# Accumulated low parts, 128-column causal matmuls and GpSimd-issued moves in a two-layer attention and recurrence trunk

## Chip, cores and metric

The kernel runs on one core of a Trainium2 chip. The metric is the device time of one execution in microseconds (us). The engines are TensorE (PE, with its weight loads listed as PEld), VectorE (DVE), ScalarE (ACT), GpSimd (POOL) and SyncE (SP).

## What is computed

Two layers over 256 tokens of width 1024, in float32. Cut to what matters:

```python
h = rmsnorm(x, norm_g[l])
q, k, v, ga, iq, ik, iw, xr, gr, ma, mb = jnp.split(h @ w_in[l], offsets, axis=-1)
q, k, iq, ik = rotary position encoding of each
# indexer: 16 heads of 64, one shared key
dots = jnp.einsum('bqhd,bsd->bqhs', iqb, ik)
idx_score = jnp.einsum('bqh,bqhs->bqs', iwb, jax.nn.relu(dots))
idx_score = jnp.where(causal, idx_score, -inf); _, sel = lax.top_k(idx_score, 64)
# attention over the selected causal keys, 8 heads of 128
p = softmax(where(selected, q @ k.T * scale, -inf));  attn = p @ v
y_a = (attn * jax.nn.silu(ga)) @ w_out_attn[l]
xr = causal_depthwise_conv(xr, conv_w[l], conv_b[l])          # width 4
r, i = sigmoid(blockdiag(xr, w_rg) + b_rg), sigmoid(blockdiag(xr, w_ig) + b_ig)   # 16 blocks of 88
hr = associative scan of (exp(-8 r softplus(-lam)), sqrt(1 - a^2) * i * xr)
y_b = (hr * jax.nn.silu(gr)) @ w_out_rnn[l]
x = x + (sigmoid(ma) * y_a + sigmoid(mb) * y_b) @ w_o[l]      # after two layers: a last rmsnorm
```

## The kernel before

**Products.** Every float32 matrix product is made of three matmuls in the fp32r type: with w = wh + wl and x = xh + xl (a rounded high part and the rest), PE computes xh·wh, xl·wh and xh·wl. So each 128x128 block of weights is loaded and streamed against 256 token columns (or the other way about, with 512 weight columns) three times. The weights come in chunks of 8 blocks (512 KB). SP loads a chunk from DRAM into `raw` (`Stream.load`, line 519, 4 buffers); ACT, or now and then DVE, rounds it into `wh` (`copy`, lines 480 and 482); DVE subtracts, wl = raw − wh (`sub`, line 486). `wh` and `wl` are rings of 6 chunks each. `Stream.chunk` is the place.

**Order.** `Program` (from line 232) is a scheduler that runs when the kernel is built: each operation has a cost and a latency, and it writes out one fixed order for each engine. PE's order follows the units of `plan` (line 65), with parts shifted later by the LATE constants; the other engines go by deadlines that follow from PE's positions. Once built, an instruction waits for its data and for the instructions ahead of it on its own engine.

**A layer.** `plan` sets: the head unit (indexer key `ik`, head weights `iw`, three indexer query groups), the other indexer queries `iq`, then for each of 11 groups of recurrence channels the units xr, gr and gate, mixed with the gates ga, ma, mb; then four pairs of q, k (and twice v) with attention, then yb, ya and the output projection wo.

**The indexer.** `rotate` (line 773) makes the rotary encoding of the projection in PSUM: it first copies the 32-partition halves crosswise into `sw` (four ACT copies of 32x512 for `iq`, line 473), then two products and a sum on DVE. `queries` (line 853) splits the result `iqr` of two groups (four heads) into two stacks `iqs` of 128 partitions, one head's high part over its low part: two 64-row copies and two 64-row subtractions. `head` makes `kh` and `kl` of the key on rows 0 to 63 and again on 64 to 127. `dots` (line 871) multiplies a stack with kh and with kl, always over all 256 keys, for both halves t of the queries; ACT's relu into `rl` and DVE's weighted sum into `wk` follow, and POOL masks what is not causal. `select` finds the top 64.

**The gates.** The recurrence blocks are 88 wide and the tiles 128, so `gather` (line 975) collects the foreign rows of neighbouring tiles into `xf` and `xk` by SBUF-to-SBUF transfers that SP issues (line 991), between its weight loads; `gate` multiplies them.

**Attention.** `logits` (line 1082) multiplies q and k for both query halves over all 256 keys. `attend` (line 1108) transposes the three causal blocks of probabilities into `ptp`, splits them into `pth` and `ptl` of 512 columns whose first 128 are a zero block, and multiplies `v` with 256 columns for both key halves st, the zero block included. `v` (line 1067) is made in eight units before the first and third pair.

Of the kernel before, what the change touches and what calls it, by code (L numbers as in the profile page):

```python
# [64 lines left out]
def plan(l):  # L65
# [21 lines left out]
    for pr in range(4):  # L87
        u += [("q", 2 * pr), ("q", 2 * pr + 1), ("k", 2 * pr), ("k", 2 * pr + 1)]
        if pr % 2 == 0:
            u += [("v", pr // 2, c) for c in range(4)]  # L90
        u.append(("attn", pr))
# [56 lines left out]
NCH = -(-NBLK // 8)  # L148

# [76 lines left out]
ENGINES = ("pe", "act", "dve", "pool", "dma")  # L226
LATENCY = {"pe": 190.0, "act": 140.0, "dve": 130.0, "pool": 200.0, "dma": 2000.0}
# [4 lines left out]
class Program:  # L232
# [52 lines left out]
    def issue(self):  # L285
# [27 lines left out]
        table = None  # L313
        order = []
# [3 lines left out]
        while n < total:  # L318
# [19 lines left out]
            for h in o.new:  # L338
                k = (h.pool, h.tag)
                slots[k].pop(0)  # L340
                given[k][h.index] = True
                while nalloc[k] < len(given[k]) and given[k][nalloc[k]]:
                    nalloc[k] += 1
            o.start, o.end = s, s + cost
# [49 lines left out]
    def choose(self, e, cand, free, slots, nalloc, given, table, pepos):  # L394
# [3 lines left out]
        for o in cand:  # L398
# [15 lines left out]
            if e == "act" and o.tabs is not ANY and table not in o.tabs:  # L414
                pr += TABLE_LAG
                if o.prio[0] > pepos + URGENT:
                    s = max(s, o.ready + HOLD)
            key = (s if s > now else now, pr, o.no)
# [7 lines left out]
TABLE_LAG = 10000.0  # L426
URGENT = 8000.0
# [5 lines left out]
def trunk(ctx, tc, xT, pos, pre, par, fgb, wst, out):  # L433
# [34 lines left out]
    def act(o, i, func, **kw):  # L468
        c = (50 if i.psum() else 94) + 0.833 * o.size() + (200 if "accum_out" in kw else 0)
        aps = [kw[k] for k in ("scale", "bias") if isinstance(kw.get(k), V)]  # L470
        outs = [o] + ([kw["accum_out"]] if "accum_out" in kw else [])
        pg.op("act", c + 93 * len(aps), outs, [i] + aps,
              lambda: nc.scalar.activation(real(o), real(i), func, **{k: real(v) for k, v in kw.items()}),
              TABS.get(func))
# [39 lines left out]
    def trans(o, i):  # L514
        pg.op("pe", 70, [o], [i, ident], lambda: nc.tensor.transpose(real(o), real(i), real(ident)))
# [12 lines left out]
    class Stream:  # L528
# [23 lines left out]
        def chunk(self, c):  # L552
            if c not in self.parts:
# [14 lines left out]
                copy(wh, raw)  # L568
                sub(wl, raw, wh.bitcast(F32))
# [63 lines left out]
    for i in range(2):  # L633
        ph = const(f"pth{i}", [512], F32R)
        pl = const(f"ptl{i}", [512], F32R)
        pset(ph.bitcast(F32)[:, 0:128], 0.0)
        pset(pl.bitcast(F32)[:, 0:128], 0.0)
        pts.append((ph, pl))
# [133 lines left out]

    def rotate(o, ps, sw, tabs, step):
# [11 lines left out]
    class Layer:  # L785
        def __init__(self, l, xg, norm):
# [6 lines left out]
            self.rope = {}  # L793
            self.aT = []
# [14 lines left out]
        def head(self):  # L809
# [12 lines left out]
            rotate(ikr[:64], ps[:64], f1("sw")[:64], [t[:64] for t in self.ti], 32)  # L822
            mul(iwt, ps, R)
            kh, kl = self.kh, self.kl
            for b in (0, 64):
                copy(kh[b:b + 64], ikr[:64])
            for b in (0, 64):
                sub(kl[b:b + 64], ikr[:64], kh.bitcast(F32)[:64])
# [24 lines left out]
        def queries(self, i):  # L853

            iqr = f2("iqr")
            rotate(iqr, self.banks["iq"], f2("sw"), [t.twice() for t in self.ti], 32)
            st = [r2("iqs") for _ in range(2)]
            for a in range(2):
                s = slice(64 * a, 64 * a + 64)
                copy(st[a][s], iqr[s])  # L860
            for a in range(2):
                s = slice(64 * a, 64 * a + 64)
                d = slice(64 - 64 * a, 128 - 64 * a)
                sub(st[a][d], iqr[s], st[a].bitcast(F32)[s])
# [6 lines left out]
        def dots(self, i, st, t):  # L871

            pg.late = LATE_DOTS
            ps = bank("pq", "dots")
            for a in range(2):
                w = st[a][:, t * P:t * P + P]
                mm(ps[:, a, :], w, self.kh, True, False)
                mm(ps[:, a, :], w, self.kl, False, True)
            pg.late = 0.0
            n = P * (t + 1)  # L880
# [94 lines left out]
        def gather(self, kind, rows):  # L975
# [8 lines left out]
            else:  # L984
                dst = pg.tile(fp, "f1", [P, T], F32R, nm("xk"), F1)
                for h in range(2):
# [3 lines left out]
            pg.op("dma", 300 * len(moves), [dst], list(src.values()),  # L990
                  lambda: [nc.sync.dma_start(real(o.bitcast(F32)), real(i.bitcast(F32))) for o, i in moves][-1])
# [75 lines left out]
        def v(self, n, c):  # L1067
            ps = self.by_token("v", self.h[2 * c:2 * c + 2], c == 0, c == 3)
            if c == 3:
                self.vt = []  # L1070
                for t in range(2):
                    self.vt.append((r2("vh").join(), r2("vl").join()))
                    split(self.vt[t], ps[t])
# [8 lines left out]
        def logits(self, hd):  # L1082
# [3 lines left out]
            for t in range(2):  # L1086
                s = slice(t * P, t * P + P)
                mm(ps[:, t, :], qh[:, a, s], kh[:, a, :], True, False)
                mm(ps[:, t, :], qh[:, a, s], kl[:, a, :], False, False)
                mm(ps[:, t, :], ql[:, a, s], kh[:, a, :], False, True)  # L1090
# [17 lines left out]
        def attend(self, hd, lts):  # L1108
            pg.late = LATE_LOG + LATE_TURN
            ps = bank("pt", "ptp").join()  # L1110
            for dst, lt, s in ((384, 1, 0), (128, 1, P), (256, 0, 0)):
                trans(ps[:, dst:dst + P], lts[lt][:, s:s + P])
            ph, pl = pts[hd % 2]
            act(ph[:, P:], ps[:, P:], AF.Copy)
            sub(pl[:, P:], ps[:, P:], ph.bitcast(F32)[:, P:])
# [4 lines left out]
            for st in range(2):  # L1120
                vh, vl = self.vt[st]
                r = slice(256 - 256 * st, 512 - 256 * st)
                c = slice(a * P, a * P + P)
                for w, m in ((vh, ph), (vh, pl), (vl, ph)):
                    mm(ps, w[:, c], m[:, r], n == 0, n == 5)
# [194 lines left out]
```

## Time and profile before

| | |
|---|---|
| median of 3 runs | 706.12 us (705.9 to 706.37) |
| profiled execution | 705.1 us, of which the span in the profile is 703.3 us |
| PE busy | 686.1 us, 98% of the span, 4720 matmuls |
| DVE busy | 602.6 us, 86% |
| ACT busy | 482.8 us, 69% |
| POOL busy | 6.4 us, 1% |
| transfers | 125.24 MB, 178 GB/s mean |
| TensorE clock granted | 1.00 of 2.4 GHz throughout |

The profile is of one execution. "Busy" is time in which an instruction of that engine was running. A matmul's row has its start and a length; matmuls overlap, so the distance between two starts says how long one occupies PE. An arrow `<-` behind a wait names the engine and tile whose end released it.

### The profile page before, as it was taken

The numbers are of one execution on the slowest core, as the hardware profiler recorded it, in microseconds if no ns is written. First come the engines' busy times: TensorE is split into PE (matmuls) and PEld (weight loads), VectorE is DVE, ScalarE is ACT, GpSimd is POOL, SyncE is SP. The second block draws the span as 40 slices with busy tenths as digits, with TensorE's granted clock in tenths as the row PEclk, the third lists the DMA queues.
The fourth block names the chain that finished last, engine by engine and source line by source line (L and its number), as shares of the span: only waits on it lengthen the run. The fifth ranks groups of instructions, "written<-read, shape, count | busy, mean of one in ns | idle before, by whom it ended". The sixth has DMA issues, their size and how long they took to land.

```text
span 703.3 us, 12628 instructions
## 1 busy us (share of the span) xinstructions
PE 686.1 (98%) x4720; PEld 638.4 (91%) x4720; DVE 602.6 (86%) x1177; ACT 482.8 (69%) x775; POOL 6.4 (1%) x18
## 2 busy tenths in 40 slices
PE   7898999999999999999999999999999999999996
PEld 7898999999999998888999899999999898988885
DVE  7989999999897959857779997999989987796573
ACT  7996675799995748444558766588769765674433
POOL 0000000000000000000000000000000000000000
PEclk9999999999999999999999999999999999999999
DMA  8646566667756462655553655576666565535621
GB/s 292 195 157 211 159 197 201 203 189 220 223 177 189 149 192 75 205 180 179 173 173 111 213 178 163 177 220 207 210 205 185 182 190 163 180 101 171 195 73 60
DMA packets 38104, 125.24 MB, mean 178 GB/s; under 512 B 4892, under 2 KB 7260, under 8 KB 38044
## 3 DMA queue, kind: packets, MB, share of 16 engines
q1 hardware_dynamic: 38044, 124.44, 56.5%
q8 instruction: 37, 0.61, 0.3%
q14 instruction: 23, 0.19, 0.1%
HBM read 119.77 MB, written 1.05 MB: 172 GB/s over the span
## 4 chain that ended last, share of the span: by engine, by line
PE 82%; DVE 7%; ACT 6%; issue 2%; DMA 2%; SPq 0%; DVEq 0%; ACTq 0%
PE rps L512 14%; PE yb L512 9%; PE q L512 7%; PE k L512 7%; PE ops L512 6%; PE ma L512 6%; PE ya L512 6%; PE v L512 6%; PE gps L512 5%; PE ga L512 4%; PE mb L512 4%; DVE wl L486 2%; PE iq L512 2%; ACT wh L480 2%; PE lg L512 2%
## 5 line engine op out<-in xcount | busy, mean ns | idle before, releaser
L486 DVE TENSOR_TENSOR wl<-raw,wh 128x1024 fp32r<-128x1024 f32 x223 | 271.5, 1220 | 58.4 <-ACT wh L480 57.1
L480 ACT ACTIVATE wh<-raw 128x1024 fp32r<-128x1024 f32 x196 | 207.3, 1059 | 138.6 <-PE rps L512 21.4
L512 PE MATMUL rps<-hh,wh 128*128 128x256 f32 x352 | 99.5, 283 | 0.0
L512 PE MATMUL rps<-hl,wh 128*128 128x256 f32 x352 | 99.5, 283 | 0.0
L512 PE MATMUL rps<-hh,wl 128*128 128x256 f32 x352 | 99.5, 283 | 0.0
L512 PEld LDWEIGHTS rps<-hh,wl 128*128 128x128 f32 x352 | 67.4, 192 | 0.3
L512 PEld LDWEIGHTS rps<-hh,wh 128*128 128x128 f32 x352 | 67.3, 191 | 0.3
L512 PEld LDWEIGHTS rps<-hl,wh 128*128 128x128 f32 x352 | 67.4, 191 | 0.0
L512 PE MATMUL yb<-wh,g 128*128 128x512 f32 x176 | 59.0, 396 | 0.0
L512 PE MATMUL iq<-xg,wh 128*128 128x256 f32 x232 | 45.3, 285 | 0.0
L512 PE MATMUL ya<-wh,aT 128*128 128x512 f32 x128 | 40.8, 395 | 0.0
L512 PE MATMUL ga<-hh,wh 128*128 128x256 f32 x128 | 36.3, 283 | 2.0 <-DVE iwt L486 2.0
L512 PEld LDWEIGHTS iq<-xg,wh 128*128 128x128 f32 x232 | 37.4, 192 | 0.0
L512 PEld LDWEIGHTS yb<-wh,g 128*128 128x128 f32 x176 | 32.5, 188 | 5.3
L512 PE MATMUL q<-hh,wl 128*128 128x256 f32 x128 | 36.4, 284 | 0.0
L512 PE MATMUL q<-hh,wh 128*128 128x256 f32 x128 | 36.3, 284 | 0.0
L512 PE MATMUL ga<-hl,wh 128*128 128x256 f32 x128 | 36.3, 283 | 0.0
L512 PE MATMUL k<-hh,wl 128*128 128x256 f32 x128 | 36.3, 283 | 0.0
L512 PE MATMUL q<-hl,wh 128*128 128x256 f32 x128 | 36.2, 283 | 0.0
L512 PE MATMUL ga<-hh,wl 128*128 128x256 f32 x128 | 36.2, 283 | 0.0
L512 PE MATMUL k<-hh,wh 128*128 128x256 f32 x128 | 36.2, 283 | 0.0
L512 PE MATMUL k<-hl,wh 128*128 128x256 f32 x128 | 36.2, 283 | 0.0
(264 smaller groups left out, 1944.6 us busy)
## 6 DMA issues: line engine op xcount, KB each, us to landing
raw<-in_wst_dram SPq DMA_DIRECT2D x224, 512.0 KB, 4.0
xk<-xs SPq DMA_DIRECT2D x24, 48.0 KB, 3.5
out_dram<-z SPq DMA_DIRECT2D x4, 256.0 KB, 2.3
rah<-in_wst_dram SPq DMA_DIRECT2D x2, 256.0 KB
xr<-in_xT_dram SPq DMA_DIRECT2D x1, 512.0 KB
fg<-in_fgb_dram SPq DMA_DIRECT2D x2, 256.0 KB
xk<-xs SPq DMA_DIRECT2D x8, 40.0 KB
xf<-xs SPq DMA_DIRECT2D x2, 160.0 KB
```

Of the source, the lines that this page charges most:

```text
L480: lambda: nc.scalar.activation(real(o), real(i), AF.Copy),
L486: lambda: nc.vector.tensor_tensor(real(o), real(a), real(b), op=op))
L512: lambda: nc.tensor.matmul(real(o), real(w), real(m), start=start, stop=stop, skip_group_check=grp))
```

## The change

The line numbers of the rows below that are headed "now" are of the changed kernel.

- **Low parts.** For 38 of the weight chunks (every third one before the first q of each layer, 19 a layer; `SUMMED`) DVE no longer subtracts. ACT writes wl = −raw, rounded, and a transfer that GpSimd issues loads the same chunk from DRAM a second time and adds it to wl on arrival.
- **128 columns.** `dots` and `logits` of query half t = 0 multiply the first 128 keys only, and `attend` multiplies key half st = 1 with the second 128 queries only. The zero block of `pth` and `ptl`, and its four memsets, are gone.
- **Indexer.** `rotate32` copies the projection once (ACT, 128x512) and swaps the 32-row quarters by four transfers on GpSimd's queue. `queries` makes one copy and one subtraction of 128x512 and moves 64-row halves by three transfers; `kh` and `kl` are made once and moved to the other 64 rows by two.
- **Gathers.** The gates' transfers are issued by GpSimd instead of SP.
- **v.** The second four v units go between the units of pair 1 instead of behind those of pair 2.
- **Scheduler.** A kind of operation "sum" for the transfers on GpSimd, costs of 2000 and 700 a transfer and a latency of 3500; PE's matmuls are given at least 110 each less a reserve of up to 60, and short ones are pushed apart; a transpose counts 112 instead of 70.

```diff
         u += [("q", 2 * pr), ("q", 2 * pr + 1), ("k", 2 * pr), ("k", 2 * pr + 1)]
-        if pr % 2 == 0:
-            u += [("v", pr // 2, c) for c in range(4)]
+        if pr == 0:
+            u += [("v", 0, c) for c in range(4)]
+        if pr == 1:
+            u[-4:] = [w for c, w in enumerate(u[-4:]) for w in (("v", 1, c), w)]
...
+def summed_chunks():
+    out, n = set(), 0
+    for l in range(L):
+        early = sum(len(unit_blocks(u)) for u in plan(l)[:plan(l).index(("q", 0))])
+        out.update(range(n // 8 + 6, (n + early) // 8, 3))
+        n += sum(len(unit_blocks(u)) for u in plan(l))
+    return out
+SUMMED = summed_chunks()
...
 PSUM_TAGS = ("pp", "pq", "pt")
-ENGINES = ("pe", "act", "dve", "pool", "dma")
-LATENCY = {"pe": 190.0, "act": 140.0, "dve": 130.0, "pool": 200.0, "dma": 2000.0}
+ENGINES = ("pe", "act", "dve", "pool", "dma", "sum")
+LATENCY = {"pe": 190.0, "act": 140.0, "dve": 130.0, "pool": 200.0, "dma": 2000.0, "sum": 3500.0}
...
                     nalloc[k] += 1
+            if o.eng == "pe":
+                cost = max(cost, ISSUE - self.spare)
+                self.spare = min(max(self.spare + cost - ISSUE, 0.0), SPARE)
...
                     s = max(s, o.ready + HOLD)
+            if e == "pe" and o.cost < ISSUE:
+                pr += -SHORT if self.spare >= ISSUE - o.cost - 5.0 else SHORT
...
 TABLE_LAG = 10000.0
+ISSUE = 110.0
+SPARE = 60.0
+SHORT = 6000.0
...
     def trans(o, i):
-        pg.op("pe", 70, [o], [i, ident], lambda: nc.tensor.transpose(real(o), real(i), real(ident)))
+        pg.op("pe", 112, [o], [i, ident], lambda: nc.tensor.transpose(real(o), real(i), real(ident)))
...
                 wl = pg.tile(wp, "wl", [P, 1024], F32R, nm("wl"), WBUF)
-                copy(wh, raw)
-                sub(wl, raw, wh.bitcast(F32))
+                if c in SUMMED:
+                    pg.op("act", 94 + 0.833 * 1024, [wl], [raw],
+                          lambda: nc.scalar.activation(real(wl), real(raw), AF.Copy, scale=-1.0))
+                    copy(wh, raw)
+                    pg.op("sum", 2000, [wl], [wl],
+                          lambda: nc.gpsimd.dma_start(real(wl), wst[c], accum_op=OP.add))
+                else:
+                    copy(wh, raw)
+                    sub(wl, raw, wh.bitcast(F32))
...
+    def move(moves):
+        outs, ins = ({a.h: a for a in side}.values() for side in zip(*moves))
+        pg.op("sum", 700 * len(moves), list(outs), list(ins),
+              lambda: [nc.gpsimd.dma_start(real(o.bitcast(F32)), real(i.bitcast(F32))) for o, i in moves][-1])
+    def rotate32(o, ps, sw, tabs):
+        n = o.shape[0]
+        act(o, ps, AF.Copy, also=(sw,))
+        move([(sw[b:b + 32], o[b ^ 32:(b ^ 32) + 32]) for b in range(0, n, 32)])
+        mul(o, o, tabs[0])
+        mul(sw, sw, tabs[1])
+        add(o, o, sw)
...
             ikr, iwt = f1("ikr"), f1("iwt")
-            rotate(ikr[:64], ps[:64], f1("sw")[:64], [t[:64] for t in self.ti], 32)
+            rotate32(ikr[:64], ps[:64], f1("sw")[:64], [t[:64] for t in self.ti])
...
             kh, kl = self.kh, self.kl
-            for b in (0, 64):
-                copy(kh[b:b + 64], ikr[:64])
-            for b in (0, 64):
-                sub(kl[b:b + 64], ikr[:64], kh.bitcast(F32)[:64])
+            split((kh[:64], kl[:64]), ikr[:64])
+            move([(t[64:], t[:64]) for t in (kh, kl)])
...
             iqr = f2("iqr")
-            rotate(iqr, self.banks["iq"], f2("sw"), [t.twice() for t in self.ti], 32)
-            st = [r2("iqs") for _ in range(2)]
-            for a in range(2):
-                s = slice(64 * a, 64 * a + 64)
-                copy(st[a][s], iqr[s])
-            for a in range(2):
-                s = slice(64 * a, 64 * a + 64)
-                d = slice(64 - 64 * a, 128 - 64 * a)
-                sub(st[a][d], iqr[s], st[a].bitcast(F32)[s])
+            rotate32(iqr, self.banks["iq"], f2("sw"), [t.twice() for t in self.ti])
+            one, low, two = r2("iqs"), r2("iql"), r2("iqs")
+            split((one, low), iqr)
+            move([(two[:64], one[64:]), (two[64:], low[64:])])
+            move([(one[64:], low[:64])])
+            st = one, two
...
             ps = bank("pq", "dots")
+            n = P * (t + 1)
...
                 w = st[a][:, t * P:t * P + P]
-                mm(ps[:, a, :], w, self.kh, True, False)
-                mm(ps[:, a, :], w, self.kl, False, True)
+                mm(ps[:, a, :n], w, self.kh[:, :n], True, False)
+                mm(ps[:, a, :n], w, self.kl[:, :n], False, True)
             pg.late = 0.0
-            n = P * (t + 1)
...
                         moves.append((dst[d:d + z - a], src[i][a:z, h, :]))
-            pg.op("dma", 300 * len(moves), [dst], list(src.values()),
-                  lambda: [nc.sync.dma_start(real(o.bitcast(F32)), real(i.bitcast(F32))) for o, i in moves][-1])
+            move(moves)
...
             if c == 3:
-                self.vt = []
+                self.vt[n] = [(r2("vh").join(), r2("vl").join()) for _ in range(2)]
                 for t in range(2):
-                    self.vt.append((r2("vh").join(), r2("vl").join()))
-                    split(self.vt[t], ps[t])
+                    split(self.vt[n][t], ps[t])
...
             for t in range(2):
-                s = slice(t * P, t * P + P)
-                mm(ps[:, t, :], qh[:, a, s], kh[:, a, :], True, False)
-                mm(ps[:, t, :], qh[:, a, s], kl[:, a, :], False, False)
-                mm(ps[:, t, :], ql[:, a, s], kh[:, a, :], False, True)
+                s, n = slice(t * P, t * P + P), P * (t + 1)
+                mm(ps[:, t, :n], qh[:, a, s], kh[:, a, :n], True, False)
+                mm(ps[:, t, :n], qh[:, a, s], kl[:, a, :n], False, False)
+                mm(ps[:, t, :n], ql[:, a, s], kh[:, a, :n], False, True)
...
             ps = bank("pt", "ptp").join()
-            for dst, lt, s in ((384, 1, 0), (128, 1, P), (256, 0, 0)):
+            for dst, lt, s in ((2 * P, 1, 0), (0, 1, P), (P, 0, 0)):
                 trans(ps[:, dst:dst + P], lts[lt][:, s:s + P])
+            ps = ps[:, :3 * P]
             ph, pl = pts[hd % 2]
-            act(ph[:, P:], ps[:, P:], AF.Copy)
-            sub(pl[:, P:], ps[:, P:], ph.bitcast(F32)[:, P:])
+            act(ph, ps, AF.Copy)
+            sub(pl, ps, ph.bitcast(F32))
...
             n = 0
-            for st in range(2):
-                vh, vl = self.vt[st]
-                r = slice(256 - 256 * st, 512 - 256 * st)
+            for st, r in ((0, slice(P, 3 * P)), (1, slice(0, P))):
+                vh, vl = self.vt[hd // 4][st]
...
                 for w, m in ((vh, ph), (vh, pl), (vl, ph)):
-                    mm(ps, w[:, c], m[:, r], n == 0, n == 5)
+                    mm(ps[:, st * P:], w[:, c], m[:, r], n == 0, n == 5)
...
             mul(of, ps, self.sga[hd])
```

PE issues as many matmuls as before: 160 of them (32 of `dots`, 24 of `logits` and 24 of `attend` in each layer) go from 256 to 128 columns. POOL's list has 144 transfers in 163 rows where it had none in 22, SP's 239 rows instead of 307. DVE makes 185 subtractions into wl instead of 223 and rounds 49 chunks instead of 27, ACT 174 instead of 196.

On POOL, in layer 0, from the swap of the third pair of indexer query groups on, POOL's list is now as follows (sw: swapped quarters; iqs and iql: high and low parts; kh, kl: the key; wl: an accumulated low part). The memsets and masks of before had no transfer among them.

```order
L805 DMA sw_628<-iqr_614 32x512 x4
L805 DMA iqs_669<-iqs_623 64x512
L805 DMA iqs_669<-iql_657 64x512
L805 DMA sw_693<-iqr_680 32x512 x4
L805 DMA kh_710<-kh_710 64x256
L805 DMA kl_716<-kl_716 64x256
L805 DMA iqs_750<-iqs_673 64x512
L805 DMA iqs_750<-iql_707 64x512
L805 DMA iqs_623<-iql_657 64x512
L598 DMA wl_731<-in_wst_dram 128x1024
```

The first stack for `dots`, iqs_623, is complete only behind the two moves of the key and the two of the second pair's stack iqs_750.

On DVE, in the same stretch, the rows up to the key's low part kl were, before:

```order
L486 TENSOR_TENSOR iqr_629<-iqr_629,sw_531 128x512
L486 TENSOR_TENSOR wl_695<-raw_543,wh_603 128x1024
L486 TENSOR_TENSOR iqs_698<-iqr_629,iqs_698 64x512
L486 TENSOR_TENSOR iqs_704<-iqr_629,iqs_704 64x512
L486 TENSOR_TENSOR sw_311<-sw_311,si_518 64x256
L486 TENSOR_TENSOR iqr_726<-iq_505,ci_434 128x512
L486 TENSOR_TENSOR ikr_449<-ikr_449,sw_311 64x256
L486 TENSOR_TENSOR wl_733<-raw_566,wh_660 128x1024
L486 TENSOR_TENSOR kl_744<-ikr_449,kh_736 64x256
L486 TENSOR_TENSOR wl_751<-raw_607,wh_677 128x1024
```

and now:

```order
L511 TENSOR_TENSOR wl_636<-raw_468,wh_569 128x1024
L511 TENSOR_TENSOR iqr_474<-iqr_474,sw_509 128x512
L511 TENSOR_TENSOR iql_657<-iqr_326,iqs_623 128x512
L511 TENSOR_TENSOR ga_634<-ga_634,ga_461 128x512
L511 TENSOR_TENSOR sw_316<-sw_316,si_580 64x256
L511 TENSOR_TENSOR wl_683<-raw_548,wh_659 128x1024
L511 TENSOR_TENSOR ikr_307<-ikr_307,sw_316 64x256
L511 TENSOR_TENSOR iql_707<-iqr_474,iqs_673 128x512
L511 TENSOR_TENSOR kl_716<-ikr_307,kh_710 64x256
```

Two pairs of queries stand ahead of kl now where three and part of a fourth stood, and behind kl there is one subtraction where there were two.

On PE, the first products of `dots` in layer 0 were, before:

```order
L512 MATMUL dots_771<-kh_736,iqs_584 128x256
L512 MATMUL rps_756<-hh_426,wh_603 128x256
L512 MATMUL dots_771<-kl_744,iqs_584 128x256
L512 MATMUL rps_756<-hh_426,wl_695 128x256
L512 MATMUL dots_771<-kh_736,iqs_592 128x256
L512 MATMUL rps_756<-hl_441,wh_603 128x256
```

and now:

```order
L537 MATMUL dots_826<-kh_710,iqs_623 128x128
L537 MATMUL rps_794<-hh_452,wh_602 128x256
L537 MATMUL rps_794<-hh_452,wl_586 128x256
L537 MATMUL rps_794<-hl_476,wh_602 128x256
L537 MATMUL dots_826<-kl_716,iqs_623 128x128
L537 MATMUL rps_794<-hh_452,wh_602 128x256
```

A `dots` product of half t = 0 is 128 columns wide now, and three or more products of the recurrence input (rps) stand between two such.

## Rows read from the trace of the kernel before

**Rows 1.** The page, busy time, share of the span and instructions of each engine.

```profile
PE 686.1 (98%) x4720; PEld 638.4 (91%) x4720; DVE 602.6 (86%) x1177; ACT 482.8 (69%) x775; POOL 6.4 (1%) x18
```

**Rows 2.** Windows: stretch, length, busy time by engine, granted clock, DMA share, GB/s.

```profile
28.60:63.00 34.40, 29.78 (x221) 27.86 (x220) 31.76 (x50) 30.48 (x46) 0.00 (x0) 1.00 0.49 162
63.00:200.00 137.00, 136.93 (x1011) 130.54 (x1011) 131.29 (x288) 109.86 (x181) 2.48 (x4) 1.00 0.65 198
200.00:330.00 130.00, 130.00 (x795) 116.27 (x795) 103.01 (x207) 77.82 (x127) 0.00 (x0) 1.00 0.53 167
...
540.00:703.30 163.30, 157.05 (x935) 138.85 (x933) 123.20 (x241) 89.61 (x148) 0.00 (x0) 1.00 0.47 146
```

**Rows 3.** What PE waited for: total us, times, longest us.

```profile
PE pk L512 <- ACT whh L480: 5.1, 1, 5.1
PE ga L512 <- DVE iwt L486: 2.0, 1, 2.0
PE dots L512 <- DVE kl L486: 1.5, 1, 1.5
PE dots L512 <- ACT rl L473: 1.5, 2, 1.1
PE mb L512 <- DVE ga L486: 0.7, 1, 0.7
```

**Rows 4.** Chain that ended last: start, us; products of 256 (rps) and 512 (v) columns.

```profile
104.99 5.76 PE rps L512 x48
...
206.58 10.91 PE v L512 x48
```

**Rows 5.** Timeline of PE around three transposes: start, us, instruction, count.

```profile
232.80 0.49 PE L515 MATMUL ptp<-ident,lt 128*128 128x128 f32 x3
...
233.25 0.28 PE L512 MATMUL q<-hh,wl 128*128 128x256 f32 x1
```

**Rows 6.** Timeline: weight loads of eight one-column products; SP's issue of a raw load.

```profile
13.11 0.98 PEld L512 LDWEIGHTS nps<-ones,nsq 128*128 128x128 f32 x8
...
14.11 0.33 SPq L519 DMA_DIRECT2D raw<-in_wst_dram  x1
```

**Rows 7.** Groups of weight loads: count, busy us, mean ns of one, idle before.

```profile
L512 PEld LDWEIGHTS k<-hh,wh 128*128 128x128 f32 x128 | 24.5, 191 | 0.0
...
L512 PEld LDWEIGHTS nps<-ones,nsq 128*128 128x128 f32 x16 | 2.2, 191 | 0.0
```

**Rows 8.** Groups of DVE and ACT: count, busy us, mean ns of one, idle before.

```profile
L486 DVE TENSOR_TENSOR wl<-raw,wh 128x1024 fp32r<-128x1024 f32 x223 | 271.5, 1220 | 58.4 <-ACT wh L480 57.1
L480 ACT ACTIVATE wh<-raw 128x1024 fp32r<-128x1024 f32 x196 | 207.3, 1059 | 138.6 <-PE rps L512 21.4 <-PE ya L512 20.3 <-PE yb L512 19.2
...
L473 ACT ACTIVATE sw<-iq 32x512 f32<-32x512 f32 x32 | 18.9, 590 | 1.6 <-PE iq L512 1.0
L482 DVE CAST wh<-raw 128x1024 fp32r<-128x1024 f32 x27 | 18.6, 690 | 6.1 <-PE iq L512 1.7 <-PE ga L512 1.3 <-PE rps L512 1.3
...
L486 DVE TENSOR_TENSOR iqs<-iqr,iqs 64x512 fp32r<-64x512 f32 x16 | 11.0, 686 | 1.0 <-ACT iqs L480 0.6
```

**Rows 9.** Timeline: key of layer 0, key and first indexer product of layer 1.

```profile
15.73 0.16 DVE L508 RECIPROCAL sd<-sd 128x2 f32<-128x2 f32 x1
...
57.46 0.42 DVE L486 TENSOR_TENSOR kl<-ikr,kh 64x256 fp32r<-64x256 f32 x1
...
398.99 0.42 DVE L486 TENSOR_TENSOR kl<-ikr,kh 64x256 fp32r<-64x256 f32 x1
...
399.35 0.28 PE L512 MATMUL dots<-kh,iqs 128*128 128x256 f32 x1
```

**Rows 10.** The page, DMA issues: KB each, median us from issue to landing.

```profile
raw<-in_wst_dram SPq DMA_DIRECT2D x224, 512.0 KB, 4.0
xk<-xs SPq DMA_DIRECT2D x24, 48.0 KB, 3.5
```

**Rows 11.** Timeline of SP's queue: four gathers in a row, us for the four.

```profile
83.92 3.08 SPq L991 DMA_DIRECT2D xk<-xs  x4
```

## What the change does to the time: a prediction

> **What bounds the kernel now.** I read the busy line first [rows 1]: PE works in 98% of the span, DVE in 86%, ACT in 69%, POOL hardly. PE is the bound on the whole, so the next question is whether it is the bound everywhere. The windows [rows 2] say nearly so: from 63 to 200 us PE idles 0.07 of 137 us, from 200 to 330 us not at all, and the granted clock reads 1.00 in each. What is lost lies at the start, between 28.6 and 63 us (34.40 − 29.78 = 4.6 us) and at the tail, which the change does not touch. The waits of PE [rows 3] name the rest: 5.1 us for the first weights (untouched), and 2.0 + 1.5 + 1.5 + 0.7 = 5.7 us at ga, dots and mb, which the change can give back. So there are two possible gains: fewer PE nanoseconds for 160 matmuls, and up to 5.7 us of waits. A shorter DVE or ACT list gives nothing by itself.
>
> **What 128 columns save.** In full streams 48 products of 256 columns take 5.76 us, 120 ns each, and 48 of 512 take 10.91 us, 227 ns each [rows 4]. A straight line through the two has 107 ns for 256 columns more, so 128 columns would be 120 − 53 = 67 ns, and 160 × 53 = 8.5 us saved. That is the upper bound. The rows nearest to the new case say something else. Between two products of q, three 128-column transposes and one 256-column product take 233.25 − 232.80 = 0.45 us; less 0.12 that is 0.33, or 110 ns a transpose [rows 5]. Transposes may stream more slowly than fp32r products, so I look at what has next to nothing to stream: eight products of one column, whose weight loads start (0.98 − 0.19) / 7 = 113 ns apart [rows 6]. The load, not the stream, sets that pace, and an fp32r weight load is as long as those, 191 ns in both groups [rows 7]. Each of the 160 matmuls still loads its own 128x128 weights, so I take 111 ns: 160 × (120 − 111) = 1.4 us. The lower bound is nothing; a loss is excluded, since both rows lie below 120 ns.
>
> The Trainium skill (TensorE: Matmul & The Clock Gate, section Back-to-back issue gap) gives about 81 ns per matmul at N = 128 in a stream of weight loads and matmuls; by it the 160 would save some 6.2 us. No row of fp32r at 128 columns exists here to decide.
>
> **Low parts by accumulation.** DVE loses 38 subtractions of 1220 ns and gains 22 roundings of 690 ns: −46.4 + 15.2 = −31 us; ACT gains 38 − 22 = 16 passes of 1059 ns, +17 us, and loses 32 quarter copies of 590 ns, −19 us [rows 8]. Both stay below PE, so this is worth nothing directly. The price of an accumulating load is in no row. It moves 512 KB as the raw loads do, which land in 4.0 us [rows 10]; from that to twice it, 8.0, is my bracket. The ring of six gives cover: the negative copy can start when the chunk six earlier is released, which is five chunks before its own use, and a chunk is 24 products of 120 ns, 2.88 us, so 14.4 us. Less 1.06 for the copy and 8.0 for the landing, 5 us are left. Traffic rises by 38 × 0.524 = 19.9 MB of 125; the window that holds most of it ran at a DMA share of 0.65 [rows 2]. I cost it at nothing; if the cover went, PE would stall at the next weight chunk.
>
> **Gathers, zero block, v, scheduler.** SP gets rid of the gathers, at 3.08 us for four [rows 11], 0.77 each, and so does its queue of weight loads; PE idled nowhere for either. The zero block's matmul columns are in the count above. The v units move within the window from 200 us, where PE was never idle and DVE was busy 103 of 130 us [rows 2]. All three: nothing.
>
> **The waits.** The ga wait is for the bank that DVE's iwt product frees. In DVE's list that product now stands 34th where it stood about 51st, so it goes; behind it the low parts of the normalized input come due, and I keep 0.8 of the 2.0: −1.2. DVE's ga product, for which mb waits, has several us less of DVE's work ahead of it, by the count that follows: −0.7. The relus of half t = 0 follow products spread over several others, so PE asks for their banks later: half of 1.5, −0.8 (bounds 0 and −1.5).
>
> The wait for kl is the one that is replaced. In layer 0, DVE's list from the norm's reciprocal (15.73 us) to the end of kl (57.88) [rows 9] loses five subtractions into wl (6.1), net four subtractions and a copy of the 64-row stacks (3.1), four rotary steps of 0.68 (2.7) and the second kl (0.4), 12.3 us; it gains a rounding (0.7) and eleven table steps (about 3.0, the wide ones priced as the 0.42 of the 256-column kl): 8.6 us less, kl at 49.3. But then five transfers on POOL's list stand before the first product: kh, kl, two into iqs_750 and one into iqs_623. Issued on SP such a one takes 0.77 [rows 11], and the last lands in 3.5 [rows 10]: 49.3 + 3.85 + 3.5 = 56.65. PE used to ask for kl at about 56.2 (57.88 less the 1.5 waited and some 0.2 to pass it on); 0.8 us of products more stand ahead of it in its list now and 1.9 of waits are gone, so 55.1. Stall 1.55, against 1.5: nothing gained. In layer 1 kl came just in time (399.41 against a first product at 399.35 [rows 9], kl itself being needed one product pair later). There DVE loses five subtractions (6.1), four stack steps (2.7), three rotary steps (2.1), a ga product (0.7) and a kl (0.4), 12.0 us, and 5.0 us of products fewer stand ahead of it in PE's list: slack 7.0, against 3.85 + 3.5 = 7.35: a new stall of 0.35. The bounds for a transfer on POOL are 0.33 us (SP's issue of one load of raw [rows 6]) and twice 0.77.
>
> **Sum**: −1.4 − 1.2 − 0.7 − 0.8 + 0.05 + 0.35 = −3.7 us. Against the profiled execution (span 703.3 plus 1.8 around it = 705.1) that is 701.4; the median of the runs lies 1.0 higher, so I forecast **702.4**.
>
> **Rival 1: the line holds.** If a 128-column fp32r product behind longer ones really takes 67 ns, the matmuls save 8.5 us and the sum is −10.8: 695.3. For it: the two rates of [rows 4] lie on a line, and the new order keeps the short ones apart, so that a load might run ahead. Against it: in [rows 5] the transposes stood among longer products as well and took 110 each, and the load of the one-column products never came faster than 113.
>
> **Rival 2: the moves come late, and it is slower.** Place: POOL's list before the first dots of each layer. With x us a transfer on POOL, the stalls are 49.3 + 5x + 3.5 − 55.1 = 5x − 2.3 in layer 0 and 5x + 3.5 − 7.0 = 5x − 3.5 in layer 1; with the other gains (−4.1) and the old kl wait (−1.5) the change is 10x − 11.4. It is nil at x = 1.14, loses over 0.2% from x = 1.28, and at 1.6 gives 710.7. For it: no transfer was ever issued by GpSimd here, the 32-row swaps and the accumulating loads stand in the same list, and everything behind a late one is late. Against it: SP's 0.77 is the only row for such an issue, and 1.28 is 1.7 times it.
>
> The Trainium skill (SBUF — State Buffer, section SBUF: two separate sides) warns that GpSimd cannot write the descriptors of its transfers while DVE runs a two-port operation such as an fp32 copy within SBUF. By it DVE's 49 roundings could each hold up a transfer, where SP's would have gone through. No run so far shows it; of [rows 8] the 690 ns of a rounding against 1220 for a subtraction of the same width fit an operation that uses two ports.
>
> **Rival 3: nothing to measure.** The waits change places (the low parts take over ga's 2.0, the relus stay) and only the 1.4 us and mb's 0.7 remain, within 0.2% of 706.12, that is 1.4 us either way (about what a measurement can tell): 704.7 to 707.5.
>
> **How the numbers follow.** My forecast (699.5 to 704.7) gets 0.55: its terms come from rows, but the waits depend on a static order timed to a few hundred nanoseconds. The line gets 0.19, slower by late moves or by an accumulated chunk that misses its use 0.15, nothing 0.11. The range 694.0 to 709.0 takes in the line's 695.3 and the slower cases up to x = 1.43; beyond lie about half of the slower cases and a few of the line's, some 0.12. Faster: 0.55 + 0.19 = 0.74; same 0.11; slower 0.15.
>
> **What would show it.** Right: starts of dots, lg and av products of 128 columns some 111 ns from the next product's; waits for iwt, ga and rl shrunk; a wait of 1 to 2 us at the first dots, now ended by a transfer into iqs; DVE near 570 us, ACT near 480; no wait of PE for wl. The line would show as 67 ns starts. Rival 2 would show long gaps between transfers on POOL's queue, and PE waiting for iqs, kh or kl for over 4 us in all. The prediction is wrong if PE waits for wl between 63 and 200 us, or for xk and xf at the gates: then GpSimd's queue is the new bound, at a place that I cost at nothing.

## The result and the profile after

The changed kernel takes 718.43 us (median; 715.81 to 718.54) against 706.25, a ratio of 1.0159 (95% interval 1.0132 to 1.0187): slower by some 11 us, outside the range and on the other side. One more execution took 3838.7 us, with each matmul some four times as long; it is left out everywhere, and the profile shown is of a repeat (e1), whose profiled execution took 719.14 us.

The page of the changed kernel: span, busy time, and the rows of granted clock and DMA share in 40 slices.

```profile
span 717.3 us, 12846 instructions
...
PE 692.5 (97%) x4720; PEld 644.1 (90%) x4720; DVE 568.7 (79%) x1151; ACT 472.9 (66%) x754; POOL 118.1 (16%) x196
...
PEclk9997999999999999999999899999999999999999
DMA  8989788999956555456579988899997555534521
...
q1 hardware_dynamic: 34128, 120.83, 52.5%
q0 software_dynamic: 10656, 29.18, 20.0%
...
wl<-in_wst_dram POOLq DMA_DIRECT2D x38, 512.0 KB, 8.2
sw<-iqr POOLq DMA_DIRECT2D x32, 64.0 KB, 6.7
iqs<-iql POOLq DMA_DIRECT2D x16, 128.0 KB, 7.7
```

DVE and ACT fell about as forecast [rows 1], yet PE is busy 6.4 us longer with fewer columns: its clock dips, here visible in two slices. A move into iqs lands in 7.7 us (median from issue to landing), where the sum had 3.5 [rows 10]. What PE waits for [rows 3]:

```profile
PE dots L537 <- DMA iqs<-iql: 10.5, 2, 7.5
PE pk L537 <- ACT whh L505: 5.3, 1, 5.3
PE ga L537 <- ACT hh L505: 1.4, 1, 1.4
PE ga L537 <- DVE hl L511: 0.2, 1, 0.2
```

The waits for iwt, rl and ga's product are gone, as forecast; the waits at dots are 7.5 and 3.0 us, one a layer, instead of 1.5 for kl and 1.5 for rl. All of PE's waits are 17.4 us instead of 10.8. The windows (columns as in [rows 2]) of the first indexer stage, of the wait in it, and of the three stretches that ran at the low clock:

```profile
28.60:63.00 34.40, 28.64 (x199) 26.86 (x197) 29.02 (x56) 27.01 (x39) 13.53 (x24) 0.94 0.95 264
...
60.00:62.50 2.50, 0.00 (x0) 0.00 (x0) 2.50 (x5) 2.45 (x5) 1.79 (x3) 0.92 1.05 300
62.50:65.00 2.50, 0.00 (x0) 0.00 (x0) 2.50 (x5) 1.96 (x3) 0.31 (x1) 0.50 1.06 215
65.00:70.00 5.00, 3.44 (x16) 3.47 (x17) 0.78 (x2) 1.06 (x1) 0.73 (x2) 0.50 1.02 301
...
34.80:38.20 3.40, 3.40 (x18) 3.40 (x18) 2.80 (x10) 3.40 (x5) 2.91 (x5) 0.50 0.89 219
62.20:72.30 10.10, 5.74 (x27) 5.77 (x28) 5.43 (x13) 5.12 (x8) 3.11 (x6) 0.50 0.96 237
406.90:413.60 6.70, 6.40 (x19) 5.46 (x20) 3.37 (x7) 1.92 (x4) 1.73 (x3) 0.50 1.05 296
```

The DMA share of the stage is 0.95 instead of 0.49. PE stood still from 59.0 to 66.6 us and then ran at 0.50, that is at 1.2 GHz, until about 72; the same follows the 3.0 us wait of layer 1, and the 1.4 us wait at ga, which ended at 33.3. PE worked 3.40 + 5.74 + 6.40 = 15.5 us at 0.50. At 1.00 that work would have taken half as long, so an estimate of the clock's price is 7.8 us. With the 6.6 us more of waits that is about what separates the two spans, 717.3 and 703.3. On POOL (start, us, count, idle before and its releaser):

```profile
51.49 0.51 POOL L805 DMA_DIRECT2D sw<-iqr  x1 [1.35 <-ACT iqr L498]
53.20 0.50 POOL L805 DMA_DIRECT2D sw<-iqr  x1 [1.21 <-DMA wl<-in_wst_dram]
54.13 1.09 POOL L805 DMA_DIRECT2D sw<-iqr  x2 [0.43 <-DMA sw<-iqr]
55.66 0.52 POOL L805 DMA_DIRECT2D kh<-kh  x1 [0.44 <-ACT wh L505]
56.59 0.52 POOL L805 DMA_DIRECT2D kl<-kl  x1 [0.41 <-issue]
...
58.56 0.52 POOL L805 DMA_DIRECT2D iqs<-iql  x1 [0.42 <-DMA sw<-iqr]
```

Issuing one takes 0.52 us, less than the 0.77 assumed. But POOL also stops between them (1.21, 0.43 and 0.42 us in these rows), for transfers that have not landed.

### The profile page after: what moved, and what is told of

It is laid out like the page before. It is cut to its first block, busy times and chain, and to the rows that moved or that the text cites. A ratio compares the mean times of both kernels' runs of the same rounds, so it can differ in the third digit from the quotient of the medians.

```text
span 3836.9 us, 12846 instructions
## 1 busy us (share of the span) xinstructions
PE 3824.5 (100%) x4720; PEld 3360.3 (88%) x4720; DVE 585.5 (15%) x1151; ACT 482.8 (13%) x754; POOL 113.0 (3%) x196
## 3 DMA queue, kind: packets, MB, share of 16 engines
q1 hardware_dynamic: 34128, 120.83, 10.4%
q0 software_dynamic: 10656, 29.18, 3.9%
## 4 chain that ended last, share of the span: by engine, by line
PE 100%; ACT 0%; DMA 0%; DVE 0%; issue 0%
PE rps L537 19%; PE yb L537 9%; PE q L537 7%; PE mb L537 7%; PE ga L537 7%; PE iq L537 7%; PE v L537 7%; PE ma L537 7%; PE k L537 7%; PE ops L537 7%; PE ya L537 7%; PE gps L537 5%; PE dots L537 2%; PE lg L537 1%; PE av L537 1%; PE pk L537 1%
## 5 line engine op out<-in xcount | busy, mean ns | idle before, releaser
L537 PE MATMUL rps<-hh,wl 128*128 128x256 f32 x352 | 369.7, 1050 | 0.0
L537 PE MATMUL rps<-hl,wh 128*128 128x256 f32 x352 | 369.3, 1049 | 0.0
L537 PE MATMUL rps<-hh,wh 128*128 128x256 f32 x352 | 366.8, 1042 | 0.0
L537 PEld LDWEIGHTS rps<-hh,wh 128*128 128x128 f32 x352 | 333.4, 947 | 1.6 <-issue 1.6
L537 PEld LDWEIGHTS rps<-hh,wl 128*128 128x128 f32 x352 | 333.1, 946 | 1.6 <-issue 1.6
L537 PEld LDWEIGHTS rps<-hl,wh 128*128 128x128 f32 x352 | 333.6, 948 | 0.0
L537 PE MATMUL yb<-wh,g 128*128 128x512 f32 x176 | 280.2, 1739 | 0.0
L537 PE MATMUL iq<-xg,wh 128*128 128x256 f32 x232 | 206.7, 1046 | 0.0
L537 PE MATMUL ya<-wh,aT 128*128 128x512 f32 x128 | 199.1, 1726 | 0.0
L537 PEld LDWEIGHTS iq<-xg,wh 128*128 128x128 f32 x232 | 192.1, 946 | 0.2 <-issue 0.2
```

Source lines behind the costliest of these rows:

```text
L537: lambda: nc.tensor.matmul(real(o), real(w), real(m), start=start, stop=stop, skip_group_check=grp))
```

## The experiments

The theories: **Q**, later called **M**, the moves come late and the clock falls behind PE's wait; **S**, the accumulating loads delay; **C**, the short matmuls lower the clock. Edits are against the changed kernel where nothing else is said; ratios are to the kernel before, run beside each, with a 95% interval.

**e1**, the changed kernel again.

> The changed kernel again, for a profile of it at its usual time. Three theories for the time over 706 us, each with its place. Q: transfers on GpSimd's queue come late; then PE waits at the first dots of each layer (for iqs, kh or kl) or at the gates (for xk, xf), together over 4 us, and what is left of the loss is the clock after those waits. S: the accumulating loads come late; then PE waits for wl, between 63 and 200 us. C: the short matmuls lower the granted clock; then the clock reads under 1.00 in stretches with dots, lg and av and without a long wait ahead. All three: 716 to 719 us, mean clock about 0.985.

719.16 us, 1.0166 (1.0132 to 1.0199). Q's place, the dots: the rows above. No wait for wl, xk or xf. But Q has no place for the clock's fall behind the wait at ga.

**e2**, the kernel before with 128 columns alone:

```diff
-                mm(ps[:, a, :], w, self.kh, True, False)
+                mm(ps[:, a, :n], w, self.kh[:, :n], True, False)
```

and likewise in logits and attend.

> The kernel before with the 128-column matmuls alone (no zero block, the scheduler's costs as before). The prediction's 111 ns a matmul: 704.7, clock 1.00. The line's 67 ns: 697.6. Theory C: slower than 706 at a clock under 1.00. Theories Q and S: between 697 and 706.

703.78 us, 0.9961 (0.9946 to 0.9976). C falls: the clock of e2's four runs, 0.995 to 0.997, is within that of the kernel before in its runs (0.995 to 0.999; the 1.00 ahead of the prediction is of one profiled execution). 160 matmuls gave 2.8 us, twice the 1.4 of 111 ns a piece and far from the line's 8.5.

**e3**, no accumulating loads:

```diff
-SUMMED = summed_chunks()
+SUMMED = set()
```

> The changed kernel with DVE's subtraction for every chunk (no accumulating load). Theory S: 702 or less. Theory Q: most of the loss stays, 710 to 718, with the waits at dots or at the gates. Theory C: the loss stays, 714 to 720.

708.67 us, 1.0029 (1.0013 to 1.0045): outside both ranges. The accumulating loads are worth 9.7 us (1.0166 − 1.0029 of 706), but PE still waits 7.5 us at the first dots, so both theories hold a part. The rows of POOL in layer 0:

```profile
45.94 0.53 POOL L805 DMA_DIRECT2D iqs<-iqs  x1
46.46 0.52 POOL L805 DMA_DIRECT2D iqs<-iql  x1
47.41 1.96 POOL L805 DMA_DIRECT2D sw<-iqr  x4 [0.43 <-ACT iqr L498]
49.55 0.52 POOL L805 DMA_DIRECT2D kh<-kh  x1 [0.19 <-issue]
50.09 0.52 POOL L805 DMA_DIRECT2D kl<-kl  x1
51.64 0.52 POOL L805 DMA_DIRECT2D iqs<-iqs  x1 [1.04 <-DMA iqs<-iqs]
53.60 0.52 POOL L805 DMA_DIRECT2D iqs<-iql  x1 [1.45 <-DMA iqs<-iql]
55.50 0.52 POOL L805 DMA_DIRECT2D iqs<-iql  x1 [1.38 <-DMA sw<-iqr]
```

and its chain that ended last, the two longest pieces there:

```profile
47.41 7.81 DMA sw<-iqr
...
55.50 7.69 DMA iqs<-iql
```

The ninth transfer from 45.94 starts when the first has landed, the tenth with the second, the eleventh with the third: each waits for the one eight places ahead of it. So where each takes 6 to 8 us to land, the queue passes on one in a microsecond or two, however short the issue. Whether the queue or the program's own semaphores set this limit, the runs do not show. These holds cost 1.04 + 1.45 + 1.38 = 3.9 us, the landing 4.2 more than the 3.5 assumed. The timeline of PE shows the short matmuls at full clock:

```profile
71.25 0.22 PE L537 MATMUL dots<-kh,iqs 128*128 128x128 f32 x1
71.30 0.45 PE L537 MATMUL mb<-wh,hl 128*128 128x512 f32 x1
71.58 0.22 PE L537 MATMUL dots<-kl,iqs 128*128 128x128 f32 x1
...
71.93 0.39 PE L537 MATMUL dots<-kh,iqs 128*128 128x128 f32 x2
72.16 0.40 PE L537 MATMUL mb<-wl,hh 128*128 128x512 f32 x1
```

One costs 71.58 − 71.25 − 0.227 = 0.10 us between longer ones, and 0.23 / 2 = 0.115 in a pair: in these rows keeping them apart gains 15 ns at most.

**e4**, 256 columns and the zero block again.

> The changed kernel with dots, logits and av back at 256 columns and the zero block. Theory C: 702 to 706, clock 1.00. Theories Q and S: as slow as the changed kernel or slower by 1 to 8 us, clock still under 1.00.

716.58 us, 1.0157 (1.0117 to 1.0197): as slow. C is out. The 2.8 us of e2 do not show here: with 128 columns (e1) the ratio is 1.0166, and the intervals overlap. PE also waits 2.3 us for accumulated chunks here.

**e5**, the scheduler told of the landing:

```diff
-LATENCY = {"pe": 190.0, "act": 140.0, "dve": 130.0, "pool": 200.0, "dma": 2000.0, "sum": 3500.0}
+LATENCY = {"pe": 190.0, "act": 140.0, "dve": 130.0, "pool": 200.0, "dma": 2000.0, "sum": 8000.0}
```

> The changed kernel with one number changed: the scheduler counts 8.0 us instead of 3.5 for a transfer issued by GpSimd (7.7 us is what the moves into iqs took to land in the changed kernel's trace). PE's list then has the first dots 5.7 us later in layer 0 and 9.8 us later in layer 1. Theory M (the loss is PE's wait for the moved stacks and the clock of 1.2 GHz behind that wait): wait at dots under 3 us instead of 10.5, clock 1.00, 702 to 706. Theory S (the accumulating loads fill the DMA engines, and every load is late): the clock and the dots may recover but PE waits for wl or at ga, 712 or more.

717.69 us, 1.0162 (1.0142 to 1.0182). M falls. S's range and its waits are met (1.9 us at ga for hh, 2.0 for wl, though for low parts that DVE makes), but neither dots nor clock recovered: PE still waits 6.9 us for the moves, which land in 9.8 us now, and its busy time is 692.6 us. A later place doesn't help while the transfers get later too.

**e6 and e7**, rotate, queries and kh/kl as before, in e6 with the accumulating loads and in e7 without them.

> The changed kernel with the indexer as before (ACT's quarter copies, 64-row stacks on ACT and DVE), accumulating loads and GpSimd's gathers kept. Theory M: no wait for a transfer at dots, clock 1.00, 701 to 705. Theory S: most of the loss of 10.5 us that went with the accumulating loads stays, 710 or more.

> The changed kernel with the indexer as before and DVE's subtraction for every chunk: what is left is 128 columns, gathers issued by GpSimd, v and the scheduler. Both theories: 702 to 705, as the 128 columns alone (703.8). If GpSimd's queue itself is late (waits for xk or xf at the gates): 706 or more.

e6 715.37 us, 1.0129 (1.0112 to 1.0146), as S had it; e7 705.54, 0.9994 (0.9984 to 1.0003), just above its range, with no wait at the gates. The accumulating loads cost 9.5 us without a single indexer move too. PE's waits in e6:

```profile
PE pk L537 <- ACT whh L505: 5.6, 1, 5.6
PE ga L537 <- DVE iwt L511: 3.4, 1, 3.4
PE dots L537 <- ACT sw L498: 2.8, 1, 2.8
PE mb L537 <- ACT kh L505: 2.4, 1, 2.4
PE iq L537 <- DMA wl<-in_wst_dram: 1.2, 1, 1.2
PE mb L537 <- DVE iqr L511: 1.0, 1, 1.0
PE dots L537 <- DVE kl L511: 0.8, 1, 0.8
```

Only the fifth names an accumulated chunk; the others are DVE and ACT coming late. They sum to 17.2 us, against 10.5 in e7, and PE is busy 689.2 us against 685.9. e7 is 2.3 us above e2 (1.3 either way); which of the gathers on GpSimd, the v units and the scheduler's constants costs it was not tried apart.

**e8**, e3 with all moves issued by SP:

```diff
-              lambda: [nc.gpsimd.dma_start(real(o.bitcast(F32)), real(i.bitcast(F32))) for o, i in moves][-1])
+              lambda: [nc.sync.dma_start(real(o.bitcast(F32)), real(i.bitcast(F32))) for o, i in moves][-1])
```

> The changed kernel without accumulating loads, all moves and gathers issued by SP instead of GpSimd, at the same places in every other engine's list. Theory G (what makes them late is that GpSimd issues them): they land in about 3.5 us as SP's gathers did before, the wait at the first dots falls from 9.3 us to under 5, 704 or less. Theory M (they are late because the DMA engines are full with weight loads then, share 1.02 to 1.06): landing stays near 6 us and the wait at 7 to 10 us, 706 to 712.

714.0 us, 1.0113 (1.0092 to 1.0134), outside both ranges and worse than e3: the waits at dots are 11.3 us instead of 9.3. So SP as issuer is no cure, but the run does not test the issuer alone. SP also issues the weight loads, four of them stand among the moves, and the last move of the first stack went out at 57.22 instead of 55.50. PE's first product followed at 62.75, so that move took some 5.5 us, less than e3's 7.69.

**e9**, e6 with the accumulating loads only behind the indexer:

```diff
-        out.update(range(n // 8 + 6, (n + early) // 8, 3))
+        out.update(range(n // 8 + 27, (n + early) // 8, 3))
```

> The kernel of e6 (indexer as before, accumulating loads) with the first 7 of the 19 accumulated chunks of each layer left to DVE's subtraction, so that no accumulating load runs before the first dots are done. Theory S1 (they cost because they fill the DMA engines in the indexer's stage, where raw loads and buffers have no time in hand): 704.5 to 707, as e7 without any (705.5), waits of PE as there. Theory S2 (every accumulating load costs something wherever it is): 12 of 19 of the 9.8 us between e6 and e7, 710 to 713.

706.38 us, 1.0002 (0.9992 to 1.0011), in S1's range. The first seven of each layer cost nearly all, the other twelve 0.6 us, though the DMA share from 63 to 200 us is 0.86 there instead of 0.66 in e7.

**e10**, e3 with the swaps issued on ACT's queue.

> The kernel of e3 (no accumulating loads) with the 32-row swaps issued on ACT's queue instead of GpSimd's; the moves of 64 rows stay on GpSimd's. In e3's trace each transfer on GpSimd's queue from the ninth on starts when the one eight places before it has landed. Theory L (this limit of eight delays the last move of the first stack): it is issued at about 52 us instead of 55.5, PE's wait at the first dots falls from 7.5 to 3 or 4 us and the time to 702 to 706. Theory M alone (landing of 6 to 8 us with full DMA engines, no limit): the wait stays at 6 to 8 us, 707 to 711.

715.49 us, 1.0129 (1.0113 to 1.0145): neither. The wait for iqs fell to 6.8 us in two (longest 3.7) and the first stack's moves were no longer held, but four issues take ACT 2.4 to 3.7 us, and what ACT makes came later: the key's move went out at 54.12 instead of 49.55.

**e13 and e14** divide the early cost. e13 is e6 with the negative copy on DVE, e14 is e7 with the negative copy on ACT kept and DVE's subtraction over it:

```diff
-                    pg.op("act", 94 + 0.833 * 1024, [wl], [raw],
-                          lambda: nc.scalar.activation(real(wl), real(raw), AF.Copy, scale=-1.0))
+                    tsc(wl, raw, -1.0, None, OP.mult)
```

> The kernel of e6 (indexer as before, 38 accumulating loads, 715.4) with the negative copy made by DVE (a product with -1) instead of ACT. Theory D (the accumulating loads cost by filling the DMA engines in the indexer's stage): still 711 or more, DMA share in 28.6 to 63 us as in e6. Theory A (they cost by the extra pass on ACT, which is nearly full in that stage): 704 to 708.

> The kernel of e7 (indexer as before, no accumulating load, 705.5) with ACT's negative copy kept for the same 38 chunks, and DVE's subtraction writing over it: the extra pass on ACT without the second load. Theory A: 711 or more, with waits for ACT at ga, mb and dots. Theory D: 704 to 708.

e13 709.38 us, 1.0037 (1.0023 to 1.0051); e14 709.37, 1.0036 (1.0026 to 1.0045). Each falls between its theories: the pass on ACT alone costs 3 us, the loads with the pass on DVE 3 us, both on ACT and the queue 9.5. Why the two together cost more than their sum is not shown. The stage's windows, first of e7, then of e14, then of e6, show both resources:

```profile
28.60:63.00 34.40, 30.54 (x217) 28.94 (x215) 31.50 (x45) 29.42 (x42) 0.00 (x0) 0.95 0.51 165
```

```profile
28.60:63.00 34.40, 30.25 (x210) 28.05 (x210) 30.77 (x47) 33.66 (x48) 0.00 (x0) 0.95 0.52 165
```

```profile
28.60:63.00 34.40, 27.62 (x189) 25.85 (x188) 28.80 (x48) 32.18 (x46) 2.58 (x3) 0.92 0.72 193
```

In e14 ACT is busy 33.66 of 34.40 us; in e6 the DMA share is 0.72 instead of 0.51, and ACT has 2.8 us more than in e7. This split is of the kernel with the indexer as before. For the change itself it was not made: there ACT is busy 27.01 of the 34.40 us, and the DMA share is 0.95.

**e15**, the change without the early accumulating loads (e9's edit).

> The changed kernel with only the first 7 accumulated chunks of each layer left to DVE's subtraction; its moved indexer stays. If what was found for the two adds up (e3 708.7 with the moves and no accumulating load, and 0.6 to 0.8 for the 12 later chunks): 708 to 711, with 7 to 10 us of waits for iqs at dots. If the later chunks hurt as well once GpSimd has the moves too: 713 or more.

709.2 us, 1.004 (1.0021 to 1.0059), with 7.7 us of waits for iqs: the moves and the later chunks add up, and the early chunks are the other 8.9 us of e1's loss.

**e11, e12, e16** look for a better version: e2 and e10 with the dots later, and e11 with all query units first.

```diff
-LATE_DOTS = 40000.0
+LATE_DOTS = 44000.0
```

> The 128 columns alone (e2) with the scheduler's LATE_DOTS 44 us instead of 40: the first dots stand 4.2 us later in PE's list in layer 0 and 3.9 in layer 1. If the waits at dots of e2 (kl 1.1, rl 0.6, kh 0.3) and the clock of 1.2 GHz behind them go: 700 to 703. If they only turn into a wait elsewhere: 703 to 705.

> The kernel of e10 with LATE_DOTS 46 us instead of 40 (first dots 3.5 us later in layer 0, 5.2 in layer 1). Theory L: the rest of the wait is covered and the clock stays at 1.00, 699 to 703. Theory M: some 3.5 us of the wait go, 704 to 708.

> The kernel of e11 (128 columns, LATE_DOTS 44 us, 702.2) with all indexer query units ahead of the first ga and mb units (NMIX 0 instead of 1), so that the normalized input has two units, 5.8 us, more before ga needs it. If the waits at ga (2.2) and mb (0.7) go and nothing takes their place: 699 to 700.5. If the relus or the banks of the query units become the wait: 702 to 705.

e11 **702.16 us, 0.9946** (0.9929 to 0.9962), which beats the kernel before and the changed one; e12 711.7, 1.0081 (1.0056 to 1.0106), outside both ranges; e16 703.05, 0.9947 (0.9933 to 0.9962), no better than e11: iwt, 4.0 us at iq now, is the wait wherever the units go. In e11 the waits for kl and kh are gone and those for rl have grown:

```profile
PE pk L512 <- ACT whh L480: 5.2, 1, 5.2
PE ga L512 <- DVE iwt L486: 2.2, 1, 2.2
PE dots L512 <- ACT rl L473: 2.1, 3, 1.1
PE mb L512 <- DVE ga L486: 0.7, 1, 0.7
```

They sum to 10.2 us, against 10.4 in e2, so the waits only changed places. What differs is PE's busy time, 683.6 us against 685.9: the profile of e2 has 3.3 us of work at 0.50 behind the waits at dots (61.7 to 65.0 us), that of e11 has none before its end. Against e2 the gain is 1.1 us in ratios, and the two intervals overlap.

## Why the prediction was wrong

In ratios to the kernel before, the change is −2.8 us for the columns (e2), +2.3 for gathers, v and scheduler (e7 − e2), +2.5 for the indexer's moves (e3 − e7) and +9.7 for the accumulating loads (e1 − e3), 11.7 in all. The second and third are known to 1.3 us either way, the last to 2.6, and taken in another order the steps may differ: e4 shows no gain from the columns.

- **128 columns**: right in kind, the size low. 0.10 to 0.115 us each, so near 111 ns and far from the line's 67; e2's gain holds 0.4 us of shorter waits as well. In e11, at the clock of the profile before, PE is busy 2.5 us less, 104 ns each. The 81 ns that the Trainium skill (TensorE: Matmul & The Clock Gate, section Back-to-back issue gap) gives does not hold for these matmuls.
- **Waits at ga, mb and rl**: right in size, 1.6 us left in e1 of 2.0 + 0.7 + 1.5, where 1.5 was forecast. That the new wait at ga ends with ACT's hh, and that the clock falls behind it, was not.
- **"I cost it at nothing"** of the accumulating loads is the step that failed worst. The cover of 14.4 us was counted for a chunk by itself; it is right that PE hardly ever waited for these chunks (0 us in e1, 1.2 in e6, 2.3 in e4). But I looked at the totals of ACT and at the DMA share from 63 to 200 us, where the price is indeed small (e9), and not at the stage from the start to 63 us, where ACT was busy 30.48 of 34.40 us [rows 2], and where five more passes and five more loads stand in e1. They made other work late: kl was ready at 52.90 in e1, at 49.75 in e3. Of the 10.4 us between the spans of e1 and e3, 2.8 are more waits of PE; most of the rest is the clock, 15.5 us of work at 0.50 against 3.2, worth 6.2 by the same estimate. The loads of 19.9 MB also kept the DMA engines longer than raw loads of as many bytes: 29.18 MB at 20.0% of 717.3 us against e3's 9.25 MB at 4.9% of 706.9 is 109 us of all 16 engines for 19.93 MB, 5.5 us a MB, where raw loads take 0.525 × 717.3 / 120.83 = 3.1.
- **"The last lands in 3.5"** is the term of the moves that failed. In e3 kl was ready at 49.75, near the 49.3 forecast, and its move issued at 50.09; then the holds took 3.9 us and the landing 7.69, and the first product came at 63.28 instead of 56.65. The 3.5 us came from gathers of 48 KB in a stretch at a DMA share of 0.65 [rows 2, rows 10]; here 128 KB moved at 1.0 and over. In the change itself (e1) kl came 3.6 us late, the last move of the first stack went out at 58.56, and layer 1's new wait was 3.0 us instead of 0.35.
- **No term for the clock.** Every stall was priced by its length. After its waits PE ran at 1.2 GHz for 15.5 us of work, some 7.8 us lost (the estimate above), more than the waits themselves added.
- **Rival 2** had the right place and the right sign, at chances of 0.15, but the wrong lever: x, the issue, was 0.52 for the moves, far under its 1.28. Their landing and the eight places did it, and its price lacked the clock too. The Trainium skill's rule on GpSimd's descriptors (SBUF — State Buffer, section SBUF: two separate sides) does show in the traces, at a small price: in e1 an accumulating load's issue took 1.44 us instead of a median of 0.93, and ended 0.09 us behind the DVE rounding that ran meanwhile. Of the moves up to the first dots none was held so. The load's issue on POOL and the rounding on DVE:

```profile
517.24 1.44 POOL L598 DMA_DIRECT2D wl<-in_wst_dram  x1
517.90 0.69 DVE L507 CAST wh<-raw 128x1024 fp32r<-128x1024 f32 x1 [1.42 <-PE rps L537]
```

## What to carry to other kernels

Cost a transfer that enters the path by its landing at the DMA share of that very stage, and add the time that its queue holds it back, instead of its issue or a landing from a quieter stage. Work taken from an engine that is not the bound brought nothing here (DVE's 34 us), and the engine that gets it must be read stage by stage: one that is 69% busy on the whole may be full where it counts. A wait of PE costs more than its length where the clock falls behind it, so the place of its consumers (e11: 4 us later, some 1 us gained, not clear of the noise) is worth a try before the data path is rebuilt.

## What the runs showed of the hardware

- Eight transfers issued by GpSimd were under way at most; the ninth's issue waited for the first to land (e1, e3). What sets the limit is not shown.
- Landing times moved with the DMA share: moves of 128 KB in e3 7.7 to 7.9 us when issued between 51 and 56 us (share 1.02 while they were under way), 3.5 to 4.2 between 73 and 80 us (0.69); gathers of 48 KB by GpSimd 3.1 us in e7 (0.66 from 63 to 200 us), 6.0 in e1 (0.92). An accumulating load took 8.2 us, a raw load of the same bytes 4.5 beside it (medians of e1).
- After PE waits of 1.4, 7.5 and 3.0 us in e1 the granted clock stood at 0.50 for 3.4, 5.7 and 6.4 us of work; the wait of 1.8 us in layer 1 of e3 and that of 2.0 us in the kernel before left it at 1.00. So the length of a wait alone does not tell in these profiles.
